# Which products of a Strassen-Winograd feed-forward block get their low weight part by an accumulating DMA

## The chip, the core and the metric

The kernel runs on one core of a Trainium2 chip. The metric is the device time in microseconds (us) of one execution: 2176.34 us before the change, the median of three runs (2171.39 to 2179.06).

Engines are called as the profile calls them: PE is TensorE, DVE is VectorE, ACT is ScalarE, POOL is GpSimd, SP is SyncE. SP issues the loads of weights, POOL the accumulating DMAs that this change is about; each has a queue of its own, and both queues use the same 16 DMA engines.

## The reference, cut to what matters

```python
# x (1, 512, 1024), DEPTH = 2 layers, D_FF = 2816, all float32
def swiglu(h, w_gu, w_down):
    gate, up = jnp.split(h @ w_gu, 2, axis=-1)
    return (jax.nn.silu(gate) * up) @ w_down

for l in range(DEPTH):
    x = x + 0.5 * swiglu(rmsnorm(x, g_ffn1[l]), w_ffn1_gu[l], w_ffn1_down[l])
    ...                       # conv heads, attention heads, cross-attention
    x = x + 0.5 * swiglu(rmsnorm(x, g_ffn2[l]), w_ffn2_gu[l], w_ffn2_down[l])
return rmsnorm(x, g_final)
```

The change touches the four feed-forward blocks (FFNs) alone: the products with w_gu (1024 x 5632, called gates) and with w_down (2816 x 1024, called down).

## The kernel before, in words

**Float32 in three passes.** PE multiplies a rounded form of float32. Each operand is therefore split into hi (the value rounded) and lo (value - hi), and each product is the sum of three matmuls, hi·hi, hi·lo and lo·hi.

**Products.** Most of an FFN is done in 2 x 2 blocks by the Strassen-Winograd scheme: seven products in place of eight, in the order `ORDER = (1, 7, 6, 2, 5, 4, 3)`. Product 1 takes the weight quadrant 11 as it is, product 2 the quadrant 21, product 3 the quadrant 22; products 7, 6, 5 and 4 take sums of quadrants, called T3, T2, T1 and T4: T3 = 22 - 12, T2 = T3 + 11, T1 = 12 - 11 (the code's signs), T4 = 21 - T2. DVE makes these sums (L83). Of the activations there are sums of the same kind.

A *gates chunk* has 512 columns of gate and as many of up; there are 20 such chunks, five to an FFN. A *unit* is the weight block of half a product, 128 x 1024 numbers, 512 KB. In the gates a unit feeds 12 matmuls with 512 moving columns (L216 in `mm3`, which other lines of the program use too). In a *down group* a unit feeds 24 matmuls with 256 moving columns (L658). There are eight big groups (two units of 24 a product) and three small ones (over three row blocks a quadrant: a unit of 24 and one of 12). Groups stand between chunks.

**Weights.** The class `Weights` brings them. `raw` lists a 512 KB load; `load` issues, on SP, as many as its limit of blocks outstanding allows, into the pool "big" of 12 buffers (L144); `free` gives a block back and calls `load`. `unit` lists a unit. `prefetch` makes the units, three ahead of the one that PE takes (`AHEAD = 3`, four buffers in the pool of units): hi by a cast on ACT (L164), then lo in one of two ways:

- on DVE: lo = source - hi (L169);
- by DMA (`keep == "dma"`): ACT writes -source into lo (L166, rounded as hi is), and POOL issues a DMA that adds the source to it in memory order (L167, `accum_op`). Its rows in the profile read wlo<-big.

Before, products 1, 2 and 3 take the second way everywhere, in gates and down groups alike: 186 accumulating DMAs.

**Order.** `ffn_plan` writes the order of chunks, transposes of activations (`turn`, L599), preparations of moving operands (`ready`) and products. `ready` makes a product's moving operand of activations: a sum on DVE (L630, L631, L637), hi by a cast on ACT (L644), lo on DVE (L645). Before, the `ready` of each product stands just ahead of the product that precedes it, and so it is issued while the product before that one runs on PE. In a big group the transposes of the next activations stand between product 1 and product 7. Each engine runs its instructions in order; semaphores between them are set by the framework, by tiles: who writes a tile waits until its readers are done, an accumulating DMA among them. An instruction that waits holds up everything behind it on its engine. A load on SP that writes a big buffer waits for the last reader of what the buffer held before.

Of the kernel before, what the change touches and what calls it, by code (L numbers as in the profile page):

```python
# [41 lines left out]
class Weights:  # L42
# [27 lines left out]
    def block(self, w, k0, nk, *cols):  # L70
        self.unit(self.raw(w, k0, nk, *cols))

    def quads(self, w, rows, cols, n):

        r, tmp = {}, {}
        parts = [(at, min(2, rows[0][1] - at)) for at in range(0, rows[0][1], 2)]

        def raw(q, h):
            at, nk = parts[h]
            r[q, h] = self.raw(w, rows[int(q[0]) - 1][0] + at, nk, (cols[int(q[1]) - 1], n))  # L80

        def tt(out, a, b, op):
            self.nc.vector.tensor_tensor(out=out, in0=a, in1=b, op=op)  # L83
            return out

        def block(q, h):
            return self.tiles[r[q, h]]

        def keep():
            pass  # L90

        def t3(h):
            tmp[h] = self.big((P, parts[h][1], n))
            return tt(tmp[h], block("22", h), block("12", h), ALU.subtract)

        def t2(h):
            return tt(tmp[h], tmp[h], block("11", h), ALU.add)

        def t1(h):
            return tt(block("12", h), block("12", h), block("11", h), ALU.subtract)  # L100

        def t4(h):
            return tt(tmp[h], block("21", h), tmp.pop(h), ALU.subtract)

        def freeing(*qs):
            return lambda: [self.free(r[q]) for q in qs]

        def product(i):
            for h in range(len(parts)):
                if i == 1:  # L110
                    raw("11", h)
                    self.unit(r["11", h], None, keep, "dma")
                elif i == 7:
                    raw("22", h)
                    raw("12", h)
                    self.unit(None, lambda h=h: t3(h), keep)
                elif i == 2:
                    raw("21", h)
                    self.unit(r["21", h], None, keep, "dma")
                elif i == 6:  # L120
                    self.unit(None, lambda h=h: t2(h), keep)
                elif i == 5:
                    self.unit(None, lambda h=h: t1(h), freeing(("11", h), ("12", h)))
                elif i == 4:
                    self.unit(None, lambda h=h: t4(h), freeing(("21", h)))
                else:
                    self.unit(r["22", h], None, freeing(("22", h)), "dma")

        return product

# [52 lines left out]
def trunk(ctx, tc, a, consts, out):  # L183
# [93 lines left out]
    for l in range(DEPTH):  # L277
        for which in (1, 2):
            gu, dn = a[f"w_ffn{which}_gu"][l], a[f"w_ffn{which}_down"][l]
            if which == 2:  # L280
                w_in, w_out = a["w_mix_in"][l], a["w_mix_out"][l]
                W.limit = 4
                for k in range(4):
                    W.block(w_in, 2 * k, 2, (2560, 512))
                for kind, i in MIX:
                    W.block(w_in, 0, KD, (MIX_COL[kind] + P * i, P))
                for c in range(KD):
                    W.block(a["w_xkv"][l], 0, KD, (P * c, P))
                for c in range(KD):
                    W.block(w_out, 0, KD, (P * c, P))  # L290
                for c in range(2):
                    for k in range(4):
                        W.block(a["w_xkv"][l], 2 * k, 2, (D + 512 * c, 512))
                W.limit = BIG_BUFS - 4
                for n in ("w_xq", "w_xo"):
                    for c in range(KD):
                        W.block(a[n][l], 0, KD, (P * c, P))
                W.slow = 10
            W.limit = BIG_BUFS - 2
            product = {}  # L300
            for op, c, i in ffn_plan(l == DEPTH - 1 and which == 2):
                if op == "plain":
                    c0 = P * FIRST[c]
                    W.block(gu, 2 * i, 2, (c0, 256), (DFF + c0, 256))
                elif op == "product":
                    if c not in product:
                        c0 = P * FIRST[c]
                        product[c] = W.quads(gu, ((0, 4), (4, 4)), (c0, DFF + c0), CHUNKS[c])
                    product[c](i)
                elif op == "group":  # L310
                    if c not in product:
                        product[c] = W.quads(dn, c, (0, 512), 512)
                    product[c](i)
                elif op == "down":
                    W.block(dn, FIRST[c], CHUNKS[c] // P, (256 * i, 256))
                elif op == "leave":
                    W.limit = 4
                    for e in range(4):
                        W.unit(W.raw(dn, FIRST[c] + 2 * (e % 2), 2, (512 * (e // 2), 512)), keep=True)
# [202 lines left out]
    def swiglu_half(n, after=None, early=None):  # L522
# [122 lines left out]
                nc.vector.tensor_tensor(out=lo, in0=o, in1=hi.bitcast(F32), op=ALU.subtract)  # L645
                made[c, i, p] = hi, lo

        def group(c, i, last):

            if i in (1, 7, 2):  # L650
                acc[CHAIN[i]] = [PS() for _ in range(2)]
# [1 line left out]
            for p, nk in pairs(c):  # L653
                w, z = W.take(), made.pop((c, i, p))
                for f in range(4):
                    for k in range(nk):
                        for q, (y, v) in enumerate(((0, 0), (0, 1), (1, 0))):
                            mm(  # L658
                                bank[f // 2][:, f % 2 * 256 : f % 2 * 256 + 256],
                                w[y][:, k, f * P : (f + 1) * P], z[v][:, k, :],  # L660
                                start=i in (1, 7, 2) and p == k == q == f % 2 == 0,
                                stop=2 * p + k == c[0][1] - 1 and q == 2,
                                skip_group_check=True,
                            )
            for half, tok in {
                1: ((0, 0),), 7: ((1, 1),), 6: ((0, 1),), 2: ((0, 0),), 5: ((1, 1),), 4: ((0, 1),), 3: ((1, 0),),
            }[i]:
                for b in range(2):
                    o = xx[2 * half + b][:, :, tok * 256 : tok * 256 + 256]
                    nc.vector.scalar_tensor_tensor(  # L670
                        out=o, in0=bank[b].rearrange("p (f t) -> p f t", f=2), scalar=0.5, in1=o,
                        op0=ALU.mult, op1=ALU.add,
                    )
# [62 lines left out]
        for at, (op, c, i) in enumerate(plan):  # L736
# [8 lines left out]
            elif op == "ready":  # L745
                ready(c, i)
            elif op == "group":
                group(c, i, after is not None and at >= len(plan) - 2 * len(ORDER))
            elif op == "down":
                down(c, i)  # L750
            else:
# [513 lines left out]
def ffn_plan(last):  # L1265
# [8 lines left out]
    def group(c, turn=None):  # L1274
# [3 lines left out]
        out.extend([("ready", c, 1), ("ready", c, 7), before, ops[0]])  # L1278
        if turn is not None:
            out.append(("turn", turn, 0))  # L1280
        for j in range(1, len(ORDER)):
            if j + 1 < len(ORDER):
                out.append(("ready", c, ORDER[j + 1]))
            out.append(ops[j])

    def both(c):

# [69 lines left out]
```

## Time and profile before

| what | value |
|---|---|
| median of three runs | 2176.34 us |
| the profiled execution | 2176.87 us, span 2175.1 us, mean granted clock 0.996 |
| PE busy | 2124.5 us, 98% |
| DVE busy | 1568.4 us, 72% |
| ACT busy | 1359.4 us, 62% |
| POOL busy | 258.9 us, 12% |
| accumulating DMAs (queue q0) | 95.17 MB, 23.8% of the 16 engines' span |
| loads (queue q1) | 212.88 MB, 31.4% of the 16 engines' span |

The span runs from the first to the last event on the core. Busy time is the sum of an engine's instructions. The releaser of a wait is what ended it. Issue to landing of a DMA is counted from the instruction that issues it to its last byte. PEclk is the granted clock of PE as a share of full speed.

### The profile page before, as it was taken

The numbers are of one execution on the slowest core, as the hardware profiler recorded it, in microseconds if no ns is written. First come the engines' busy times: TensorE is split into PE (matmuls) and PEld (weight loads), VectorE is DVE, ScalarE is ACT, GpSimd is POOL, SyncE is SP. The second block draws the span as 40 slices with busy tenths as digits, with TensorE's granted clock in tenths as the row PEclk, the third lists the DMA queues.
The fourth block names the chain that finished last, engine by engine and source line by source line (L and its number), as shares of the span: only waits on it lengthen the run. The fifth ranks groups of instructions, "written<-read, shape, count | busy, mean of one in ns | idle before, by whom it ended". The sixth has DMA issues, their size and how long they took to land. (4 is left out here: it accounts for less than half of the span.)

```text
span 2175.1 us, 30582 instructions
## 1 busy us (share of the span) xinstructions
PE 2124.5 (98%) x11602; PEld 1840.2 (85%) x11602; DVE 1568.4 (72%) x2196; ACT 1359.4 (62%) x1990; POOL 258.9 (12%) x293
## 2 busy tenths in 40 slices
PE   9999999999999999999999999999999999999998
PEld 7788989788888878898988898888888888788887
DVE  7687778668755667686886787777786547686775
ACT  7657676566544567667677666756664445576664
POOL 0111110022001011101101111101220010011010
PEclk9999999999999999999999999999999999999999
DMA  6776876123452256867757677742343422678662
GB/s 203 193 180 158 202 180 139 49 78 94 149 145 88 68 141 166 210 158 184 182 134 173 174 190 170 173 109 68 88 126 116 126 88 68 155 190 199 164 165 59
DMA packets 224186, 310.02 MB, mean 143 GB/s; under 512 B 12206, under 2 KB 128166, under 8 KB 224038
## 3 DMA queue, kind: packets, MB, share of 16 engines
q1 hardware_dynamic: 197222, 212.88, 31.4%
q0 software_dynamic: 26784, 95.17, 23.8%
q8 instruction: 91, 1.49, 0.3%
q14 instruction: 57, 0.47, 0.1%
q10 hardware_dynamic: 32, 0.01, 0.0%
HBM read 210.77 MB, written 2.10 MB: 98 GB/s over the span
## 5 line engine op out<-in xcount | busy, mean ns | idle before, releaser
L164 ACT CAST whi<-big 128x1024 fp32r<-128x1024 f32 x582 | 598.5, 1030 | 514.2 <-PE ps L216 221.0
L216 PE MATMUL ps<-whi,t 128*128 128x512 f32 x2624 | 816.2, 390 | 0.4 <-ACT t L220 0.2
L169 DVE TENSOR_TENSOR wlo<-big,whi 128x1024 fp32r<-128x1024 f32 (+1 forms) x396 | 478.1, 1207 | 222.1 <-ACT whi L164 218.0
L216 PEld LDWEIGHTS ps<-whi,t 128*128 128x128 f32 x2624 | 492.7, 188 | 102.7 <-ACT t L220 0.7
L216 PE MATMUL ps<-wlo,t 128*128 128x512 f32 x1312 | 512.4, 391 | 10.5 <-DMA wlo<-big 10.2
L216 PE MATMUL ps<-t,whi 128*128 128x512 f32 x1472 | 456.9, 391 | 1.5 <-ACT whi L855 1.5
L658 PE MATMUL ps<-t,whi 128*128 128x256 f32 x2296 | 423.6, 286 | 10.0 <-DVE t L645 7.8
L658 PEld LDWEIGHTS ps<-t,whi 128*128 128x128 f32 x2296 | 364.4, 194 | 13.3 <-DVE t L645 9.0
L658 PE MATMUL ps<-t,wlo 128*128 128x256 f32 x1148 | 327.6, 286 | 11.5 <-DMA wlo<-big 11.5
L83 DVE TENSOR_TENSOR big<-big 128x1024 f32<-128x1024 f32 x248 | 294.0, 1196 | 61.1 <-DMA wlo<-big 58.0
L216 PEld LDWEIGHTS ps<-t,whi 128*128 128x128 f32 x1472 | 274.5, 188 | 57.4 <-ACT whi L855 2.0
L167 POOL DMA_DIRECT2D wlo<-big x186 | 161.1, 866 | 1250.2 <-ACT wlo L166 636.5
L216 PEld LDWEIGHTS ps<-wlo,t 128*128 128x128 f32 x1312 | 246.4, 188 | 65.8 <-DMA wlo<-big 16.1
L216 PE MATMUL ps<-t,wlo 128*128 128x512 f32 x736 | 286.9, 390 | 1.1 <-DVE wlo L856 1.1
L658 PEld LDWEIGHTS ps<-t,wlo 128*128 128x128 f32 x1148 | 222.9, 194 | 13.1 <-DMA wlo<-big 13.1
L166 ACT ACTIVATE wlo<-big 128x1024 fp32r<-128x1024 f32 (+1 forms) x186 | 193.5, 1041 | 50.5 <-PE ps L216 49.5
L216 PEld LDWEIGHTS ps<-t,wlo 128*128 128x128 f32 x736 | 138.2, 188 | 30.5 <-DVE wlo L856 1.9
L670 DVE SCALAR_TENSOR_TENSOR x<-ps,x 128x512 f32<-128x512 f32 x154 | 103.9, 685 | 17.5 <-PE ps L658 16.9
L552 ACT COPY t<-ps 128x512 f32<-128x512 f32 x120 | 68.7, 587 | 31.0 <-PE ps L216 28.5
L926 POOL TENSOR_TENSOR t<-t,s 128x128 f32<-128x128 f32 (+1 forms) x64 | 60.2, 970 | 216.9 <-DVE s L924 182.2
L645 DVE TENSOR_TENSOR t<-t 128x512 fp32r<-128x512 f32 x88 | 57.0, 650 | 15.4 <-ACT t L644 15.1
L644 ACT CAST t<-t 128x512 fp32r<-128x512 f32 x88 | 51.1, 584 | 23.3 <-DVE t L631 15.3
(185 smaller groups left out, 1987.7 us busy)
## 6 DMA issues: line engine op xcount, KB each, us to landing
wlo<-big POOLq DMA_DIRECT2D x177, 512.0 KB, 5.1
big<-in_w_ffn_gu SPq DMA_DIRECT2D x160, 512.0 KB, 4.5
big<-in_w_ffn_down SPq DMA_DIRECT2D x80, 512.0 KB, 4.7
big<-in_w_mix_in SPq DMA_DIRECT2D x48, 512.0 KB, 4.0
big<-in_w_xkv SPq DMA_DIRECT2D x32, 512.0 KB, 3.9
big<-in_w_ffn_gu SPq DMA_DIRECT2D x32, 256.0 KB, 3.5
big<-in_w_mix_out SPq DMA_DIRECT2D x16, 512.0 KB, 4.6
big<-in_w_xq SPq DMA_DIRECT2D x16, 512.0 KB, 3.7
```

Source lines behind the costliest of these rows:

```text
L83: self.nc.vector.tensor_tensor(out=out, in0=a, in1=b, op=op)
L164: self.nc.scalar.copy(out=hi, in_=src)
L166: self.nc.scalar.activation(out=lo, in_=src, func=AF.Copy, scale=-1.0)
L167: self.nc.gpsimd.dma_start(out=lo, in_=src, accum_op=ALU.add)
L169: self.nc.vector.tensor_tensor(out=lo, in0=src, in1=hi.bitcast(F32), op=ALU.subtract)
L216: mm(ps, x, y, start=first and i == 0, stop=last and i == 2, skip_group_check=chained)
L552: nc.scalar.copy(out=s[i, e], in_=ps)
L644: nc.scalar.copy(out=hi, in_=o)
L645: nc.vector.tensor_tensor(out=lo, in0=o, in1=hi.bitcast(F32), op=ALU.subtract)
L658: mm(bank[f // 2][:, f % 2 * 256 : f % 2 * 256 + 256], w[y][:, k, f * P : (f + 1) * P], z[v][:, k, :], start=i in (1, 7, 2) and p == k == ...
L670: nc.vector.scalar_tensor_tensor(out=o, in0=bank[b].rearrange("p (f t) -> p f t", f=2), scalar=0.5, in1=o, op0=ALU.mult, op1=ALU.add,)
L926: nc.gpsimd.tensor_tensor(out=w[t], in0=w[t], in1=inv[:, t : t + 1].broadcast_to([P, (t + 1) * P]), op=ALU.mult)
```

## The change

1. `quads` takes a tuple `dma`: the products whose lo is made by the accumulating DMA. Gates chunks take (2, 3), down groups (6, 2, 5, 4, 3); every other product has its lo on DVE. In numbers: four accumulating DMAs to a gates chunk in place of six, ten to a group in place of six, 190 in all in place of 186.
2. The sums are written elsewhere. T2 goes over block 11, and T3's buffer is free from there on (before, T2 went over T3). T1 goes over block 12 as 22 - T2, T4 over block 11 as 21 - T2. Product 5 then gives back block 12 alone, product 4 blocks 21 and 11.
3. In groups, `ready` of the products 2, 5, 4 and 3 is issued in the middle of the product two before (after that product's first unit), by `group` itself. `ready` of 1, 7 and 6 stays where it was. The test for the last group counts the plan's entries anew, for `ready` entries no longer stand between the products.

The diff, without empty lines:

```diff
@@ -70,7 +70,10 @@
     def block(self, w, k0, nk, *cols):
         self.unit(self.raw(w, k0, nk, *cols))
-    def quads(self, w, rows, cols, n):
+    def quads(self, w, rows, cols, n, dma):
         r, tmp = {}, {}
         parts = [(at, min(2, rows[0][1] - at)) for at in range(0, rows[0][1], 2)]
@@ -94,37 +97,38 @@
             return tt(tmp[h], block("22", h), block("12", h), ALU.subtract)
         def t2(h):
-            return tt(tmp[h], tmp[h], block("11", h), ALU.add)
+            return tt(block("11", h), tmp.pop(h), block("11", h), ALU.add)
         def t1(h):
-            return tt(block("12", h), block("12", h), block("11", h), ALU.subtract)
+            return tt(block("12", h), block("22", h), block("11", h), ALU.subtract)
         def t4(h):
-            return tt(tmp[h], block("21", h), tmp.pop(h), ALU.subtract)
+            return tt(block("11", h), block("21", h), block("11", h), ALU.subtract)
         def freeing(*qs):
             return lambda: [self.free(r[q]) for q in qs]
         def product(i):
+            how = "dma" if i in dma else False
             for h in range(len(parts)):
                 if i == 1:
                     raw("11", h)
-                    self.unit(r["11", h], None, keep, "dma")
+                    self.unit(r["11", h], None, keep, how)
                 elif i == 7:
                     raw("22", h)
                     raw("12", h)
-                    self.unit(None, lambda h=h: t3(h), keep)
+                    self.unit(None, lambda h=h: t3(h), keep, how)
                 elif i == 2:
                     raw("21", h)
-                    self.unit(r["21", h], None, keep, "dma")
+                    self.unit(r["21", h], None, keep, how)
                 elif i == 6:
-                    self.unit(None, lambda h=h: t2(h), keep)
+                    self.unit(None, lambda h=h: t2(h), keep, how)
                 elif i == 5:
-                    self.unit(None, lambda h=h: t1(h), freeing(("11", h), ("12", h)))
+                    self.unit(None, lambda h=h: t1(h), freeing(("12", h)), how)
                 elif i == 4:
-                    self.unit(None, lambda h=h: t4(h), freeing(("21", h)))
+                    self.unit(None, lambda h=h: t4(h), freeing(("21", h), ("11", h)), how)
                 else:
-                    self.unit(r["22", h], None, freeing(("22", h)), "dma")
+                    self.unit(r["22", h], None, freeing(("22", h)), how)
         return product
@@ -305,11 +309,11 @@
                 elif op == "product":
                     if c not in product:
                         c0 = P * FIRST[c]
-                        product[c] = W.quads(gu, ((0, 4), (4, 4)), (c0, DFF + c0), CHUNKS[c])
+                        product[c] = W.quads(gu, ((0, 4), (4, 4)), (c0, DFF + c0), CHUNKS[c], (2, 3))
                     product[c](i)
                 elif op == "group":
                     if c not in product:
-                        product[c] = W.quads(dn, c, (0, 512), 512)
+                        product[c] = W.quads(dn, c, (0, 512), 512, (6, 2, 5, 4, 3))
                     product[c](i)
                 elif op == "down":
                     W.block(dn, FIRST[c], CHUNKS[c] // P, (256 * i, 256))
@@ -645,7 +649,7 @@
                 nc.vector.tensor_tensor(out=lo, in0=o, in1=hi.bitcast(F32), op=ALU.subtract)
                 made[c, i, p] = hi, lo
-        def group(c, i, last):
+        def group(c, i, last, then=None):
             if i in (1, 7, 2):
                 acc[CHAIN[i]] = [PS() for _ in range(2)]
@@ -662,6 +666,8 @@
                                 stop=2 * p + k == c[0][1] - 1 and q == 2,
                                 skip_group_check=True,
                             )
+                if then is not None and not p:
+                    ready(c, then)
             for half, tok in {
                 1: ((0, 0),), 7: ((1, 1),), 6: ((0, 1),), 2: ((0, 0),), 5: ((1, 1),), 4: ((0, 1),), 3: ((1, 0),),
             }[i]:
@@ -745,7 +751,11 @@
             elif op == "ready":
                 ready(c, i)
             elif op == "group":
-                group(c, i, after is not None and at >= len(plan) - 2 * len(ORDER))
+                j = ORDER.index(i) + 2
+                group(
+                    c, i, after is not None and at >= len(plan) - len(ORDER),
+                    ORDER[j] if 3 <= j < len(ORDER) else None,
+                )
             elif op == "down":
                 down(c, i)
             else:
@@ -1278,10 +1288,8 @@
         out.extend([("ready", c, 1), ("ready", c, 7), before, ops[0]])
         if turn is not None:
             out.append(("turn", turn, 0))
-        for j in range(1, len(ORDER)):
-            if j + 1 < len(ORDER):
-                out.append(("ready", c, ORDER[j + 1]))
-            out.append(ops[j])
+        out.append(("ready", c, ORDER[2]))
+        out.extend(ops[1:])
     def both(c):
```

**Where instructions stand now.** Three places, all in layer 0's first FFN, in the big group over chunks 2 and 3, or the one before and after it. "wlo_" is a lo of a unit, "big_" a 512 KB buffer or a sum written in one, t_ and r_ are activations; the numbers are those of tiles.

POOL's accumulating DMAs of this group, before: products 1, 2 and 3, two each.

```order
L167 DMA wlo_1861<-big_1457 128x1024
L167 DMA wlo_1904<-big_1490 128x1024
L167 DMA wlo_2077<-big_1783 128x1024
L167 DMA wlo_2116<-big_1806 128x1024
L167 DMA wlo_2297<-big_1735 128x1024
L167 DMA wlo_2342<-big_1762 128x1024
```

And of the change, products 6, 2, 5, 4 and 3:

```order
L171 DMA wlo_1970<-big_1469 128x1024
L171 DMA wlo_2046<-big_1490 128x1024
L171 DMA wlo_2083<-big_1802 128x1024
L171 DMA wlo_2114<-big_1804 128x1024
L171 DMA wlo_2154<-big_1758 128x1024
L171 DMA wlo_2190<-big_1779 128x1024
L171 DMA wlo_2230<-big_1469 128x1024
L171 DMA wlo_2266<-big_1490 128x1024
L171 DMA wlo_2311<-big_1733 128x1024
L171 DMA wlo_2344<-big_1777 128x1024
```

Product 1's two have gone, and ten stand where there were four; block buffers 1469 and 1490 occur twice, for T2 and T4.

SP's loads in the same stretch, before, with the semaphores that each waits for. DMASW0 to DMASW7 are counters that POOL's DMAs take in turn; in this group product 1 has 0 and 1, product 2 has 2 and 3, product 3 has 4 and 5, and 6 and 7 are older ones.

```order
L144 DMA big_2149<-in_w_ffn1_gu 128x2x512 [waits DMASW0_49,DMAHW3_49,DVE_49,Activation_49]
L144 DMA big_2151<-in_w_ffn1_gu 128x2x512 [waits DMASW1_49,DMAHW4_49,DVE_49,Activation_49]
L144 DMA big_2196<-in_w_ffn1_gu 128x2x512 [waits DMAHW5_49,DMASW2_49,DMAHW7_49,DVE_49,Activation_49]
L144 DMA big_2198<-in_w_ffn1_gu 128x2x512 [waits DMAHW6_49,DVE_49]
L144 DMA big_2229<-in_w_ffn1_gu 128x2x512 [waits DMAHW0_49,DMASW3_49]
L144 DMA big_2270<-in_w_ffn1_gu 128x2x512 [waits DVE_49]
L144 DMA big_2301<-in_w_ffn1_gu 128x2x512 [waits DMAHW1_49,DMASW6_49,DVE_49]
L144 DMA big_2346<-in_w_ffn1_gu 128x2x512 [waits DMAHW2_49,DMASW7_49,DVE_49]
```

And of the change, where product 6 has the counters 6 and 7, product 2 has 0 and 1, product 5 has 2 and 3, product 4 has 4 and 5, and product 3 has 6 and 7 again:

```order
L148 DMA big_2158<-in_w_ffn1_gu 128x2x512 [waits DMASW4_49,DMAHW3_49,DVE_49,Activation_49]
L148 DMA big_2194<-in_w_ffn1_gu 128x2x512 [waits DMASW5_49,DMAHW4_49,DVE_49,Activation_49]
L148 DMA big_2234<-in_w_ffn1_gu 128x2x512 [waits DMAHW5_49,DMASW0_49,DMAHW7_49,DVE_49,Activation_49]
L148 DMA big_2236<-in_w_ffn1_gu 128x2x512 [waits DMAHW0_49,DMASW1_49,DMAHW6_49,DVE_49,Activation_49]
L148 DMA big_2270<-in_w_ffn1_gu 128x2x512 [waits DMASW2_49,Activation_49]
L148 DMA big_2272<-in_w_ffn1_gu 128x2x512 [waits DMASW3_49,Activation_49]
L148 DMA big_2315<-in_w_ffn1_gu 128x2x512 [waits DMAHW1_49,DMASW4_49,Activation_49]
L148 DMA big_2348<-in_w_ffn1_gu 128x2x512 [waits DMAHW2_49,DMASW5_49,Activation_49]
```

Six loads in a row now wait for an accumulating DMA of the group's own, 0 to 5 in turn.

DVE around the moving operand of product 6, before (L630, L631 and L645 make it; L670 adds a bank of PE's sums to x; the two rows of L83 are T4's sums):

```order
L83 TENSOR_TENSOR big_1920<-big_1783,big_1920 128x1024 [waits DMAHW7_49,DVE_49]
L631 TENSOR_TENSOR t_2029<-t_2030,r_1630 128x512 [waits DVE_49]
L83 TENSOR_TENSOR big_1942<-big_1806,big_1942 128x1024 [waits DMAHW0_49]
L670 SCALAR_TENSOR_TENSOR x2_156<-ps_2045,x2_156 128x2x256 [waits PE_49]
L645 TENSOR_TENSOR t_2034<-t_2029,t_2033 128x512 [waits Activation_49]
L630 TENSOR_TENSOR t_2038<-r_1643,r_2021 128x512
L670 SCALAR_TENSOR_TENSOR x3_157<-ps_2046,x3_157 128x2x256 [waits PE_49]
L631 TENSOR_TENSOR t_2037<-t_2038,r_1643 128x512 [waits DVE_49]
L645 TENSOR_TENSOR t_2042<-t_2037,t_2041 128x512 [waits Activation_49]
```

And of the change:

```order
L635 TENSOR_TENSOR t_2026<-t_2027,r_1628 128x512 [waits DVE_49]
L86 TENSOR_TENSOR big_1469<-big_1802,big_1469 128x1024 [waits DMAHW7_49,DMASW6_49]
L649 TENSOR_TENSOR t_2031<-t_2026,t_2030 128x512 [waits Activation_49]
L634 TENSOR_TENSOR t_2035<-r_1641,r_2018 128x512
L676 SCALAR_TENSOR_TENSOR x2_156<-ps_2042,x2_156 128x2x256 [waits PE_49]
L635 TENSOR_TENSOR t_2034<-t_2035,r_1641 128x512 [waits DVE_49]
L86 TENSOR_TENSOR big_1490<-big_1804,big_1490 128x1024 [waits DMAHW0_49,DMASW7_49]
L676 SCALAR_TENSOR_TENSOR x3_157<-ps_2043,x3_157 128x2x256 [waits PE_49]
L649 TENSOR_TENSOR t_2039<-t_2034,t_2038 128x512 [waits Activation_49]
```

T4's two sums (L86, of block 21 and T2) stand there before as well, and now they wait for DMASW6 and DMASW7, product 6's accumulating DMAs, with the lo of product 6's operand (L649) behind them.

## Rows read from the trace of the kernel before

**Rows 1.** Page part 1: busy us of each engine (share of the span), instructions

```profile
PE 2124.5 (98%) x11602; PEld 1840.2 (85%) x11602; DVE 1568.4 (72%) x2196; ACT 1359.4 (62%) x1990; POOL 258.9 (12%) x293
```

**Rows 2.** What PE waited for: engine line <- releaser: us, times, longest

```profile
PE ps L658 <- DMA wlo<-big: 11.5, 8, 2.6
PE ps L216 <- DMA wlo<-big: 10.2, 11, 2.1
PE ps L658 <- DVE t L645: 7.8, 6, 1.3
...
PE ps L658 <- ACT t L644: 2.2, 4, 0.9
```

**Rows 3.** PE in L658, eleven group windows: us, busy (x), PEclk, DMA share, GB/s

```profile
332.62:367.69 35.07, 35.06 (x288) 34.76 (x288) 1.00 0.75 165
...
sum 399.45, PE 380.48 PEld 374.61; mean PE 34.59 PEld 34.06
```

**Rows 4.** Page part 5: busy us, mean ns of one | idle before, releaser

```profile
L164 ACT CAST whi<-big 128x1024 fp32r<-128x1024 f32 x582 | 598.5, 1030 | 514.2 <-PE ps L216 221.0
...
L169 DVE TENSOR_TENSOR wlo<-big,whi 128x1024 fp32r<-128x1024 f32 (+1 forms) x396 | 478.1, 1207 | 222.1 <-ACT whi L164 218.0
...
L83 DVE TENSOR_TENSOR big<-big 128x1024 f32<-128x1024 f32 x248 | 294.0, 1196 | 61.1 <-DMA wlo<-big 58.0
...
L166 ACT ACTIVATE wlo<-big 128x1024 fp32r<-128x1024 f32 (+1 forms) x186 | 193.5, 1041 | 50.5 <-PE ps L216 49.5
...
L645 DVE TENSOR_TENSOR t<-t 128x512 fp32r<-128x512 f32 x88 | 57.0, 650 | 15.4 <-ACT t L644 15.1
L644 ACT CAST t<-t 128x512 fp32r<-128x512 f32 x88 | 51.1, 584 | 23.3 <-DVE t L631 15.3
```

**Rows 5.** Page part 3: DMA queue, kind: packets, MB, share of 16 engines

```profile
q1 hardware_dynamic: 197222, 212.88, 31.4%
q0 software_dynamic: 26784, 95.17, 23.8%
```

**Rows 6.** Timeline of POOL, 1382 to 1398: start us, us, instruction [idle before]

```profile
1382.76 0.86 POOL L167 DMA_DIRECT2D wlo<-big  x1 [1.86 <-ACT wlo L166]
1385.47 0.86 POOL L167 DMA_DIRECT2D wlo<-big  x1 [1.86 <-DVE big L83]
1388.19 0.86 POOL L167 DMA_DIRECT2D wlo<-big  x1 [1.86 <-ACT wlo L166]
```

**Rows 7.** DMA issues at these three times: KB, us to landing

```profile
wlo<-big POOLq DMA_DIRECT2D x1, 512.0 KB, 5.0
...
wlo<-big POOLq DMA_DIRECT2D x1, 512.0 KB, 6.8
...
wlo<-big POOLq DMA_DIRECT2D x1, 512.0 KB, 9.0
```

**Rows 8.** Waits of SP's DMA queue, 1380 to 1390

```profile
SPq L144 <- DMA wlo<-big: 13.4, 2, 10.6
```

**Rows 9.** Windows: busy of PE, PEld, DVE, ACT, POOL, PEclk, DMA share, GB/s

```profile
1389.00:1391.00 2.00, 2.00 (x11) 1.65 (x10) 0.96 (x2) 2.00 (x3) 0.05 (x1) 1.00 1.13 228
1391.50:1392.50 1.00, 1.00 (x7) 0.84 (x6) 1.00 (x2) 0.00 (x0) 0.00 (x0) 1.00 0.99 363
```

**Rows 10.** PE's waits in 1878:1886, 2099:2108, 327:331 and 1396:1400

```profile
PE ps L216 <- DMA wlo<-big: 1.0, 1, 1.0
...
PE ps L216 <- DMA wlo<-big: 1.8, 2, 1.4
...
PE ps L658 <- DMA wlo<-big: 0.9, 1, 0.9
...
PE ps L658 <- DMA wlo<-big: 1.7, 1, 1.7
```

**Rows 11.** A gates window, all engines, 291 to 324

```profile
291.00:324.00 33.00, 33.00 (x150) 27.42 (x149) 24.04 (x28) 26.35 (x34) 5.22 (x6) 1.00 0.77 192
```

**Rows 12.** PE in L658 while its clock was at half

```profile
155.42:158.83 3.41, 3.41 (x18) 3.41 (x18) 0.50 1.03 195
```

## The prediction

> **What bounds the kernel now.** The first view is the page's busy line: TensorE (PE) is busy 2124.5 of 2175.1 us [rows 1], so the kernel ends where PE's work ends, and an edit is worth what it takes from PE's 50 us of idle time, or adds to it. The second is the list of what PE waited for [rows 2]. Read it by releaser: 21.7 us are waits for an accumulating DMA (wlo<-big: 11.5 in down groups, L658, and 10.2 in gates, L216), and 10.0 us are waits for the operand of a down group (7.8 for its lo on DVE, 2.2 for its hi on ACT). The third is PE in the down groups alone, in windows [rows 3]. An undisturbed big group runs its products 7 to 3, 288 matmuls, in 35.07 us, which is 0.1218 us a matmul and 2.92 us for a unit of 24. At that pace the eight big groups and the three small ones (252 matmuls, 30.69 us each) would take 372.6 us; they take 399.45, so 26.8 us are lost in them.
>
> **What a lo by DMA costs.** A unit's path is hi on ACT 1.03, -source on ACT 1.04, with an operand cast of 0.58 often between them [rows 4], then the DMA. The page's queue table prices the transfers [rows 5]: q0 carries only the 186 accumulating DMAs and takes 23.8% of the span of 16 engines, 2.78 us of all engines each; q1's 212.88 MB are 406 loads of 512 KB at 31.4%, 1.68 us each. So a load and an accumulating DMA together need 4.46 us of the engines, and a down unit gives them 2.92.
>
> What happens when they meet stands in one place of the trace. Accumulating DMAs are issued at 1382.76, 1385.47 and 1388.19, 2.7 us apart [rows 6], but land after 5.0, 6.8 and 9.0 us [rows 7], at 1387.8, 1392.3 and 1397.2: 4.5 and 4.9 us apart. In between SyncE waited twice for an accumulating DMA before it could issue the next load [rows 8]: each landing frees a buffer, a load starts into it, and the transfers follow each other. The throughput shows it too: 228 GB/s while one kind runs, 363 while the other does [rows 9], which is 2.30 and 1.44 us for 512 KB. That gives a lower bound of 3.74 us for the pair. The third of them kept PE waiting 1.7 us [rows 10].
>
> The Trainium skill (DMA: Bandwidth & Descriptors, Queues, rings and completion order) says that an engine changes between queues after a packet of some descriptors; the landings above follow each other as whole transfers.
>
> **Change part by part.**
>
> *Where the DMAs go.* Gates give up product 1's, 2 of 6 a chunk; down groups go from 6 (products 1, 2, 3) to 10 (6, 2, 5, 4, 3). The number hardly changes, 186 to 190, but ten now stand in a row. And the loads come to stand between them. T1 and T4 are now read by DMAs out of blocks 12 and 11, so these buffers come free at a landing: the load rows of a group wait for DMASW0 to DMASW5, the DMAs of products 2, 5 and 4, where before four of the eight waited for no DMA of their own group. So six units of each big group, from product 5's first to product 3's last, have a load in front.
>
> A unit has four buffers, so its hi starts when the unit three before it starts on PE: a lead of 8.77 us. The path is 1.03 + 0.58 + 1.04 + 5.0 = 7.65, which leaves 1.1 us. The first load finds the engines idle. The other five units each fall 4.46 - 2.92 = 1.54 us back, 7.7 in all, less 1.1: 6.6 us a group. By the lower bound of 3.74 it is 5 x 0.82 - 1.1 = 3.0. I take 5.2, nearer the upper end, since the landings seen were 4.5 and 4.9 apart. Eight groups: 41.6 us (24 to 53).
>
> By the Trainium skill's fit for one such DMA (same page, Anatomy of one DMA: about 2.0 us + bytes / 436 GB/s) 512 KB would be 3.2 us in all, an estimate, 1.2 of them transfer, and nothing would be late. The landings of 5.0 and more and the 2.78 us of [rows 5] speak against it; what it would mean is the first rival.
>
> *Small groups (three).* Their units alternate between 24 and 12 matmuls, 2.92 and 1.46 us, 4.38 a product. A first unit's lead is 2.92 + 1.46 + 1.46 = 5.84, its path at least 7.07: 1.2 us late at product 6. For products 5 and 4 the engines have 1.5 x 2.78 + 2 x 1.68 = 7.5 us of work (half a transfer taken as half the time) where PE needs 4.38: 6.2 back, less 1.1 of slack. Sum 6.3 a group, 18.9 in all (9 to 24).
>
> *Sums in other tiles.* T4 is written over block 11, which T2's DMA reads. So DVE stops at the T4 sums until product 6's DMAs land, and behind them stand an eviction and the lo of product 6's second operand: 1.20 + 0.65 us [rows 4] after the landing. Before, six big groups waited about 1.7 us at this very place (10.0 us, rows 2). I take 1.5 us in all eight, 12 us (0 to 20). T3's buffer is free earlier, which only brings two loads forward.
>
> *Operands half a product earlier.* They are made at the middle of the product two before, not at the start of the one before. PE waits only for product 6's, whose place is unchanged (behind the transposes, ahead of product 7); the others waited for nothing. Worth 0; the casts now stand between hi and lo on ACT, which is in the path above.
>
> *Product 1 on DVE.* Its waits end: 1.0 and 1.8 us in gates and 0.9 and 1.7 in groups [rows 10], with the 0.16 us that PE's pipeline hides before each of the six: -6.4 us. Price: two lo of 1.21 us a product on DVE, hidden under gates where DVE is busy 24.04 of 33 us [rows 11]; without that cover 2.4 us a chunk, and T3 of the next chunk, which waits for product 3's landing, is where it would go first. Product 2's waits in gates stay.
>
> *Clock.* PE's clock fell to half for 3.41 us four times in mid-kernel, each time within 2 us of such a wait; 18 matmuls are run there [rows 12] in place of 28: 1.2 us each. I keep that as it is (-5 to +10).
>
> **Sum.** After: 41.6 + 18.9 + 12 = 72.5 us lost in the groups, in place of 26.8: +45.7. With -6.4 it is +39.3 on the profiled execution's 2176.87 us (span 2175.1 and 1.8 around it; the median of the runs is 2176.34): **2216 us**.
>
> **Rivals.**
>
> *Faster: the DMAs hide.* If the engines took an accumulating DMA in under 2.92 us beside the loads, or served them ahead of the loads, nothing of the six units would be late. Then all DMA waits in groups end (11.5 us, which holds the 2.6 of product 1), those of product 1 in gates (2.8), half of the operand waits (5) and the clock dips (4.8): 24.1 us, **2153 us**. For it: DMA is far from busy on average, q0 and q1 together 55%, and trains of four accumulating DMAs without loads cause no wait. Against it: the landings. It decides at a spacing of 2.92 us. The skill's fit above would bring it about. 14%.
>
> *No change: it cancels.* At a spacing of 3.74, with the loads slipping behind the group's last units, a tail costs 2 us: 16 + 3 x 3.7 as now + 0 of operand waits, 27 against 26.8, less 6.4: about 2171 to 2178. 9%.
>
> *Worse: the queue behind T4.* If product 6's DMA lands with a load ahead (6.8, not 5.0 us), DVE's in-order queue stands still 1.8 us longer in each of eight groups, 14 us, and more than ten waits of over 1 us a FFN bring the clock down in each group, 11 x 1.2 = 13 us: **2243 us**. 15%.
>
> **How the numbers follow.** Forecast 62%, with a range of its own from 2185 to 2235 (24 and 53 for the tails, 9 and 24 for the small groups). Faster 14%, cancelled 9%, worse 15%. A measurement of this kernel can tell about 0.3%, 6.5 us, from no change. Faster by more: 14% and a little of the cancelled case, 0.15. Within: 0.08. Slower: 0.77. Leaving out the fast rival and the far end of the worse one, the range is 2168 to 2250.
>
> **What would show it.** Right: PE's waits in L658's successor for wlo<-big rise from 11.5 to some 55 us, in series of 1 to 1.6 us 4.4 us apart at products 4 and 3 of every group, and accumulating DMAs there land after 7 to 9 us; a big group's 288 matmuls take 41 to 42 us, a small group about 37; SyncE's loads wait for wlo<-big; no DMA wait remains in product 1. Wrong: group windows at 35 to 36 us, landings 2.9 us or less apart beside loads, or a new wait at the start of a gates chunk for a lo on DVE, which would put the cost on the cover that I counted as free.

## The result and the profile after

The changed kernel takes 2247.62 us (median of four runs, 2245.36 to 2247.77) against 2174.74 before: a ratio of 1.0327, 95% interval [1.0314, 1.034], some 73 us slower. The forecast was 2216 in a range of 2168 to 2250, so the direction and the range held (the range by 2 us at its top), but the time lies next to the worst rival's 2243. The profiled execution spans 2245.9 us, 70.8 more than before.

Where the 70.8 us are is read from two lines of each kernel. First the busy line of the page, after:

```profile
PE 2149.5 (96%) x11602; PEld 1860.7 (83%) x11602; DVE 1562.1 (70%) x2192; ACT 1361.0 (61%) x1994; POOL 262.6 (12%) x297
```

The same 11602 matmuls take PE 25.0 us more than in [rows 1], so part of the loss is no wait at all. Then what PE waited for (us in total, times, longest):

```profile
PE ps L662 <- DMA wlo<-big: 55.5, 35, 4.4
PE ps L662 <- DVE t L649: 19.2, 10, 3.1
...
PE ps L220 <- DMA wlo<-big: 2.4, 2, 1.8
...
PE ps L662 <- ACT t L648: 0.3, 1, 0.3
```

Against [rows 2]: in the groups +44.0 for the accumulating DMAs, +11.4 and -1.9 for operands; in the gates -7.8. That is +45.7, and with the 25.0 it makes the 70.7 of the span. Most of the 25.0 is the clock. PE in L662, the eleven groups one by one (us, PE busy, PEld busy, granted clock, DMA share, GB/s):

```profile
121.31:166.75 45.44, 35.23 (x252) 34.41 (x251) 0.89 0.77 180
214.77:259.75 44.98, 36.81 (x288) 34.98 (x288) 1.00 0.87 206
...
1091.01:1136.71 45.70, 38.88 (x288) 37.52 (x288) 0.93 0.96 235
...
1328.88:1372.50 43.62, 37.83 (x288) 36.40 (x288) 0.96 0.90 213
1457.70:1499.18 41.48, 36.38 (x288) 34.95 (x288) 1.00 0.95 208
...
sum 481.80, PE 406.36 PEld 393.38; mean PE 36.94 PEld 35.76
```

The sum was 399.45 with 380.48 busy [rows 3]. So the groups took 82.4 us more, 56.5 as waits (+53.5 from the list above and 2.6 that lay in product 1 of big groups before, outside these windows) and 25.9 in busy time. Where the clock column is below 1, most of that is the clock. It is not all: the groups at 214.77 and 1457.70 ran at 1.00, and PE is busy 1.8 and 1.3 us longer in them than the 35.06 of [rows 3]. It stopped five times in the second, so a stop costs about a quarter of a us of busy time beside the wait itself. The clock stood at half in 15 stretches of the trace (61.4 us together, the one at the program's end left out) in place of four (13.7 us). Each of the 15 begins in the last 1.2 us of a wait of 1.7 to 4.4 us, or within 1.6 us after one. One of them lies right behind a wait of 2.3 us in a small group:

```profile
147.07:150.48 3.41, 3.41 (x19) 3.41 (x18) 0.00 (x0) 0.00 (x0) 0.00 (x0) 0.50 1.03 173
```

PE is busy throughout, and runs 19 matmuls where 28 would have fitted.

Of what the forecast wanted to see, a big group's 288 matmuls take 41.5 to 45.7 us (41 to 42 said), a small group 41.8 to 45.4 (37 said), and product 1 waits for no DMA any more. The waits of the big groups begin earlier than said: 13.7 us stand at product 5, 7.5 at product 4 and 6.7 at product 3, the longest 3.0.

The DMAs of one big group's tail, issued from 1347 to 1370 (KB, median us to landing):

```profile
big<-in_w_ffn_gu SPq DMA_DIRECT2D x5, 512.0 KB, 10.0
wlo<-big POOLq DMA_DIRECT2D x5, 512.0 KB, 8.8
```

and the throughput there (busy of PE, PEld, DVE, ACT, POOL; clock, DMA share, GB/s):

```profile
1352.00:1356.00 4.00, 1.94 (x16) 1.73 (x15) 1.29 (x2) 3.59 (x5) 0.86 (x1) 1.00 1.06 263
1356.00:1360.00 4.00, 3.83 (x32) 3.62 (x31) 1.98 (x3) 1.52 (x2) 0.86 (x1) 1.00 1.07 218
```

The DMA engines are full, the accumulating DMAs land after 8.8 us in place of 5.1 (the page's median before), and the loads slow down as much: 10.0 us where 4.7 is the page's median (4.5 before). The two queues do not share in one way all the time. From 1357 to 1359, and then from 1364 to 1366 (packets, MB, share of the 16 engines):

```profile
q0 software_dynamic: 118, 0.42, 105.6%
q1 hardware_dynamic: 10, 0.02, 2.6%
...
q1 hardware_dynamic: 233, 0.44, 58.9%
q0 software_dynamic: 60, 0.20, 50.5%
```

The prediction had read [rows 7] as whole transfers that follow each other. The Trainium skill (DMA: Bandwidth & Descriptors, Queues, rings and completion order) has the engines change between queues in small pieces, of a packet. The second of these windows agrees with it, for both kinds move forward together there; in the first the accumulating DMAs have the engines nearly alone, though a load was issued at 1355.69 and landed only at 1365.7. What decides between the two was not found.

The other wait, at product 6, is on DVE's timeline (start, us, operation, idle before and its releaser):

```profile
1331.84 0.69 DVE L635 TENSOR_TENSOR t<-t,r 128x512 f32<-128x512 f32 x1
1335.44 1.22 DVE L86 TENSOR_TENSOR big<-big 128x1024 f32<-128x1024 f32 x1 [2.91 <-DMA wlo<-big]
1336.59 0.68 DVE L649 TENSOR_TENSOR t<-t 128x512 fp32r<-128x512 f32 x1
```

T4's sum (L86) holds DVE for 2.91 us until product 6's DMA has landed, and the lo of product 6's operand (L649) stands behind it; PE waited 2.3 us for that.

### The profile page after: what moved, and what is told of

Same layout as the page of the kernel before. It is cut to its first block, busy times and chain, and to the rows that moved or that the text cites. A ratio compares the mean times of both kernels' runs of the same rounds, so it can differ in the third digit from the quotient of the medians.

```text
span 2245.9 us, 30440 instructions
## 1 busy us (share of the span) xinstructions
PE 2149.5 (96%) x11602; PEld 1860.7 (83%) x11602; DVE 1562.1 (70%) x2192; ACT 1361.0 (61%) x1994; POOL 262.6 (12%) x297
## 5 line engine op out<-in xcount | busy, mean ns | idle before, releaser
L662 PE MATMUL ps<-t,whi 128*128 128x256 f32 x2296 | 440.7, 293 | 19.6 <-DVE t L649 19.2
L662 PEld LDWEIGHTS ps<-t,whi 128*128 128x128 f32 x2296 | 378.0, 201 | 22.8 <-DVE t L649 21.5
L662 PE MATMUL ps<-t,wlo 128*128 128x256 f32 x1148 | 340.4, 296 | 55.9 <-DMA wlo<-big 55.5
L86 DVE TENSOR_TENSOR big<-big 128x1024 f32<-128x1024 f32 x248 | 291.4, 1193 | 111.6 <-DMA wlo<-big 106.8
L220 PEld LDWEIGHTS ps<-t,whi 128*128 128x128 f32 x1472 | 274.5, 188 | 57.3 <-ACT whi L865 2.0
L662 PEld LDWEIGHTS ps<-t,wlo 128*128 128x128 f32 x1148 | 231.1, 201 | 64.1 <-DMA wlo<-big 64.0
L220 PEld LDWEIGHTS ps<-t,wlo 128*128 128x128 f32 x736 | 138.1, 188 | 30.5 <-DVE wlo L866 1.9
L391 POOL TENSOR_TENSOR s<-s,mhalf 128x4 f32<-128x4 f32 (+1 forms) x19 | 18.3, 961 | 477.2 <-DVE s L388 439.3
```

Source lines behind the costliest of these rows:

```text
L220: mm(ps, x, y, start=first and i == 0, stop=last and i == 2, skip_group_check=chained)
L662: mm(bank[f // 2][:, f % 2 * 256 : f % 2 * 256 + 256], w[y][:, k, f * P : (f + 1) * P], z[v][:, k, :], start=i in (1, 7, 2) and p == k == ...
```

## The experiments

Theory A: ten accumulating DMAs in a group share the DMA engines with the loads that they set off, product 6's hold up T4's sums on DVE, and PE's clock falls at the waits. Rivals B and C: the cost lies in the sums T, or in the earlier operands. Others are named where they are tested. Every ratio is against the kernel before on the same chip.

**One part of the change at a time.** Four kernels on the base of the one before.

The placement alone (all products get `how` as product 1 does here, and the gates' chunks take (2, 3)):

```diff
+            how = "dma" if i in dma else False
...
-                    self.unit(r["11", h], None, keep, "dma")
+                    self.unit(r["11", h], None, keep, how)
...
-                        product[c] = W.quads(dn, c, (0, 512), 512)
+                        product[c] = W.quads(dn, c, (0, 512), 512, (6, 2, 5, 4, 3))
```

> The kernel before with the new placement of accumulating DMAs alone (gates 2, 3; groups 6, 2, 5, 4, 3), sums and operands as before. Theory A (the ten DMAs of a group cost the time: they share the DMA engines with the loads that they trigger, product 6's hold up T4's sums on DVE, and PE's clock falls at the waits): 2230 to 2260 us, waits of PE in groups for wlo<-big of 45 to 65 us (55.5 in the change), for operands on DVE 14 to 24 (19.2), and ten or more falls of the clock. Here T4 is written over T2's own buffer, which product 6's DMA reads too, so T4's sums wait just as they do in the change. Rival B (the sums in other tiles make the loads wait for DMAs): 2175 to 2205. Rival C (operands made earlier delay -source on ACT): 2200 to 2225.

Measured: 2269.9 us, ratio 1.0451 [1.0434, 1.0468], more than the whole change.

```profile
PE ps L659 <- DMA wlo<-big: 59.4, 42, 4.1
PE ps L659 <- DVE t L646: 21.7, 8, 4.4
PE ps L217 <- DMA wlo<-big: 9.7, 7, 2.6
```

The placement carries all of the loss; both waits of the groups are there in full with the old sums and operands. The time is 10 us above what was expected; the gates' line shows the most of it: 9.7 us in place of the change's 2.4.

The sums alone (T1, T4 and the blocks given back as in the change):

```diff
-            return tt(tmp[h], tmp[h], block("11", h), ALU.add)
+            return tt(block("11", h), tmp.pop(h), block("11", h), ALU.add)
```

> The kernel before with the sums T written over other tiles alone; accumulating DMAs for products 1, 2, 3 as before. Theory A: within 6 us of before, 2169 to 2181. Rival B: slower by 20 us or more, since blocks 11 and 12 come free at other times and loads wait. Rival C: within 6 us.

Measured: 2179.24, ratio 1.0033 [1.0019, 1.0046]: 7 us slower, small and just clear of nothing. Rival B has fallen as the cause of 73 us.

The operands alone:

```diff
+                if then is not None and not p:
+                    ready(c, then)
```

> The kernel before with the operands of products 2, 5, 4 and 3 of the groups made half a product earlier, alone. Theory A: within 6 us of before (2169 to 2181), the waits for operands of product 6 unchanged at about 10 us. Rival B: the same. Rival C: slower by 20 us or more.

Measured: 2174.28, ratio 1.0004 [0.9994, 1.0014]: nothing. Rival C has fallen.

The gates' part of the placement alone:

```diff
-                        product[c] = W.quads(gu, ((0, 4), (4, 4)), (c0, DFF + c0), CHUNKS[c])
+                        product[c] = W.quads(gu, ((0, 4), (4, 4)), (c0, DFF + c0), CHUNKS[c], (2, 3))
...
-                        product[c] = W.quads(dn, c, (0, 512), 512)
+                        product[c] = W.quads(dn, c, (0, 512), 512, (1, 2, 3))
```

> The kernel before with product 1 of the gates on DVE alone (gates 2, 3; groups 1, 2, 3). Theory A: faster by the waits of product 1 in gates, 3 to 8 us: 2167 to 2172, no wait for wlo<-big in product 1 of a gates chunk, those in product 2 stay. Rival D (DVE was the cover and is now late in gates): slower by 5 to 48 us (up to 2.4 us in each of 20 chunks), with PE waiting for a lo on DVE.

Measured: 2172.36, ratio 0.9997 [0.9985, 1.0008]. Both expectations missed: no new wait for a lo on DVE, and no gain. The gates' waits were all in product 2 now, and the line was hardly shorter than the 10.2 of [rows 2] (the profiled execution took 2180.02 us, 8 above the median):

```profile
PE ps L217 <- DMA wlo<-big: 9.3, 8, 2.9
```

**Which of the other parts gives back 22 us.** The change with the operands made where they were:

```diff
-        out.append(("ready", c, ORDER[2]))
-        out.extend(ops[1:])
+        for j in range(1, len(ORDER)):
+            if j + 1 < len(ORDER):
+                out.append(("ready", c, ORDER[j + 1]))
+            out.append(ops[j])
```

> The changed kernel with the operands of groups made where they were before (DMA placement and sums of the change). The placement alone took 2269.9 us, the whole change 2247.6, so sums and operands together give back 22. If the operands made earlier give it back (the casts no longer stand between hi and -source of a product that is late): 2262 to 2275. If the sums do (two buffers free earlier, loads sooner): 2243 to 2253. In between, both.

Measured: 2248.15, ratio 1.0343 [1.0326, 1.036], as the whole change. So the sums in other tiles take 22 us off the new placement, though alone they cost 7. In the profiles of this run and of the placement alone, 8.6 of the 16.9 us between the spans are waits in gates (9.7 to 1.1), 7.6 waits in groups (81.1 to 73.5).

**Product 6 off the DMA.** On the change:

```diff
-                        product[c] = W.quads(dn, c, (0, 512), 512, (6, 2, 5, 4, 3))
+                        product[c] = W.quads(dn, c, (0, 512), 512, (2, 5, 4, 3))
```

> The changed kernel with product 6 of the groups on DVE again (groups 2, 5, 4, 3). Theory A: T4's sums wait for no accumulating DMA, so PE's waits for operands of product 6 fall from 19.2 to 8 to 13 us (10.0 before), the small groups' waits at product 6 (3.6, 2.9 and 2.9 us) go, waits in groups for wlo<-big fall from 55.5 to 35 to 48 us, since the tail of products 5, 4, 3 stays: 2210 to 2232 us. Rival F (product 6 is late in any case, its lo on DVE stands behind the sums): waits at product 6 stay under another name, 2240 us or more. Rival G (product 6's DMAs are the root and the tail only follows from the delay that they start): waits for wlo<-big below 25 us, under 2205.

Measured: 2215.46, ratio 1.0185 [1.0169, 1.02].

```profile
PE ps L662 <- DMA wlo<-big: 42.8, 36, 3.7
PE ps L662 <- DVE t L649: 7.7, 14, 1.3
```

32 us less. In the profiles, 36.1: 12.7 of DMA waits, 11.5 of operand waits, and 11.9 of PE's busy time, with 8 stretches of half clock in place of 15. Rivals F and G have fallen; the tail stays, as A has it.

**Loads out of the groups.** On the change; `load` does nothing while `hold` is set, from product 6 until product 4's sums are in x, and each load that was held waits for a copy of one element of x:

```diff
+            if self.late is not None:
+                self.nc.vector.tensor_copy(out=t[:, 0, :1], in_=self.late)
...
+            if i == 6 and c[0][0] != FIRST[4]:
+                W.hold = True
...
+            if i == 4:
+                W.hold, W.late = False, xx[0][:, 0, 256:257]
+                W.load()
+                W.late = None
```

> The changed kernel with the loads that the products of a group would trigger held back until product 4 has been added to x, in the eight groups that a gates chunk or down block follows within the FFN (the three groups that end an FFN keep theirs); each such load waits for a DVE copy of one element. Theory A (loads and accumulating DMAs of one group hold each other up): in these eight groups the waits for wlo<-big fall from 44 us (of 55.5; 11 are in the other three) to under 20, and the time to 2205 to 2228, some of it given back at the start of the next chunk. Rival E (ten accumulating DMAs in a row are too late by their own length and the lead of four unit buffers, loads or not): 35 us or more remain, 2238 us or more.

Measured: 2199.18, ratio 1.0115 [1.0098, 1.0132]: 48 us less than the change, below what was expected.

```profile
PE ps L667 <- DMA wlo<-big: 23.3, 20, 3.3
PE ps L667 <- DVE t L652: 17.0, 11, 2.9
...
PE ps L223 <- DVE wlo L176: 2.9, 4, 0.8
```

Of the 23.3, 12.7 are in the three groups that keep their loads. The five big groups with held loads wait 0.7 us together, where the change waited 17.4; the three small ones 9.9, where it waited 26.9. All stretches of half clock but the program's last lie in two of the three groups that keep theirs. The same big group in both kernels, all its DMAs, first the change (1328 to 1373):

```profile
q0 software_dynamic: 1440, 5.24, 59.5%
q1 hardware_dynamic: 2155, 4.15, 28.5%
...
wlo<-big POOLq DMA_DIRECT2D x10, 512.0 KB, 7.2
big<-in_w_ffn_gu SPq DMA_DIRECT2D x7, 512.0 KB, 10.0
```

and with held loads (1295 to 1340):

```profile
wlo<-big POOLq DMA_DIRECT2D x10, 512.0 KB, 4.6
big<-in_w_ffn_gu SPq DMA_DIRECT2D x9, 512.0 KB, 7.6
```

The same ten DMAs land after 4.6 us in place of 7.2 once the loads are held back. Rival E has fallen for big groups. In small groups about 3.3 us of each group's wait stay without loads, so there the row of DMAs and the short lead cost something by themselves.

**The clock.** On the change; `still` is a tile of zeros:

```diff
+            fill = {6: 24 if small else 16, 5: 16 if small else 0, 3: 24 if small else 0}.get(i, 0)
...
+                for _ in range(fill if not p else 0):
+                    mm(bank[0][:, :256], still[:, :P], still, start=False, stop=False, skip_group_check=True)
```

> The changed kernel with matmuls on zeros (added into the bank in use, so they change no value) ahead of the first unit of product 6 (24 in small groups, 16 in big) and in small groups of products 5 (16) and 3 (24): 320 matmuls, 39 us at 0.122 us each, where PE waits some 46 us in the changed kernel. Theory A (the clock falls because PE stands still there): falls of the clock go from 15 windows to 8 or fewer, and the time to 2228 to 2243 in spite of the added work. Rival H (the falls have another cause, the work filled in is simply added where it doesn't fit): 13 windows or more, and 2248 to 2290 us.

Measured: 2246.01, ratio 1.0329 [1.0313, 1.0344].

```profile
PE 2168.9 (97%) x11922; PEld 1880.2 (84%) x11922; DVE 1561.4 (70%) x2193; ACT 1361.5 (61%) x1994; POOL 262.1 (12%) x297
```

The time missed the expected range by 3 us at the top; the clock did as A says: 4 stretches at half in place of 15. The 320 added matmuls are 39.0 us, yet PE's busy time rose by only 19.4, so the clock gave back 19.6 for 47.8 us less at half; waits in groups fell from 75.0 to 52.9. The work that was filled in paid for itself, and no more.

**Can the placement be had without its costs?** Four kernels, in which loads are held, product 6 is off the DMA, or the down groups run product 2 ahead of product 6, so that the product after the transposes needs no sum of activations.

The order alone, on the kernel before (`ready` follows `DOWN`):

```diff
+DOWN = (1, 7, 2, 6, 5, 4, 3)
-        ops = [("group", c, i) for i in ORDER]
+        ops = [("group", c, i) for i in DOWN]
```

> The kernel before with the down groups' products in the order 1, 7, 2, 6, 5, 4, 3 (gates unchanged): product 2, whose operand needs no sum, comes right after the transposes, product 6 after it. Of the 10.0 us of operand waits before (all at product 6) under 4 should remain: 2162 to 2170 us. Rival: product 2's lo by DMA is now needed one product sooner with the same lead, and its wait takes the place: 2171 to 2180 us.

Measured: 2184.2, ratio 1.0049 [1.0036, 1.0062]: slower, by more than the rival said.

```profile
PE ps L659 <- DMA wlo<-big: 19.5, 15, 2.8
PE ps L217 <- DMA wlo<-big: 8.8, 9, 2.1
PE ps L659 <- DVE x L671: 8.1, 8, 1.1
```

The operand waits have gone, but the DMAs are late (11.5 to 19.5 us: 5.0 of the 8.0 more at product 2, 3.2 at product 3), and a new wait has come at product 5 in the big groups. Product 5 now follows product 6 directly and adds into the same bank, so it waits until DVE has added product 6's sums to x (L671).

The same with `hold`, whose diff stands above:

> The same, and the loads of eight groups held until product 4 is added, as in the run with held loads. Theory A: waits for wlo<-big in groups fall from 11.5 us to under 7: 2158 to 2168. Rival: three DMA products in seven leave room enough for the loads, and holding them only delays the next chunk: 2169 to 2182.

Measured: 2229.41, ratio 1.0264 [1.0248, 1.028]: far outside both.

```profile
PE ps L220 <- DMA wlo<-big: 42.2, 24, 4.3
PE ps L664 <- DMA wlo<-big: 14.7, 13, 2.6
```

The held loads now meet the accumulating DMAs of product 1 of the next gates chunk, which the change has moved to DVE: 8.8 us of waits in gates become 42.2, 34.5 of them in product 1. This is theory A once more, in another place: whatever DMA stands beside a burst of loads is late.

The change with groups (2, 5, 4, 3) and `hold`, first with the order of products as it was, then with `DOWN`; both edits stand above:

> The changed kernel with groups 2, 5, 4, 3 by DMA and held loads, order of products as it was. Theory A: product 6 on DVE takes off what it took off without held loads at the operands (from 17 to about 8 us), and the eight groups' waits for wlo<-big stay at 10 or below: 2182 to 2193 us. Rival (the two remedies take off the same thing): 2195 to 2203.

> The changed kernel with groups 2, 5, 4, 3 by DMA, held loads and the order 1, 7, 2, 6, 5, 4, 3 together. Theory A (the three costs are the loads beside the DMAs, product 6's DMAs ahead of T4's sums, and the clock at the waits; they are separate): waits for operands under 5 us, waits for wlo<-big in groups 12 to 22, six or fewer falls of the clock: 2174 to 2188 us. Rival (the tails come back in the three groups that keep their loads and at product 2, which now comes first): 2190 to 2210.

Measured: 2188.14, ratio 1.0064 [1.005, 1.0077], and 2180.32, ratio 1.0036 [1.0024, 1.0048]. Operand waits were 7.9 us in the first, and none in the second; waits for wlo<-big in groups 22.0 and, above the expected 22, 26.0. Both times lie in the ranges of theory A, though the eight groups with held loads still wait 11.7 us for wlo<-big in the first, where 10 or less was expected. The two remedies do not simply add up: held loads alone took 48 us off the change, product 6 alone 32, both together 59, so part of the loss goes with either. With loads held and product 6 on DVE the new placement comes within 16 us of the kernel before, with the other order too within 8. No kernel that was run beats it.

## Why the prediction was right in direction and short in size

- *Tails of big groups.* Right in mechanism: loads and accumulating DMAs hold each other up, shown by the run with held loads (17.4 to 0.7 us). The size was too large: 41.6 us forecast, 28.6 measured (55.5 less 26.9 in small groups), 3.6 a group where I took 5.2. Of the two bounds, the lower (3.0) was the nearer. The term that was too large is the spacing, 4.46 us, and 4.5 to 4.9 by the landings that I preferred. In the tail shown above, the DMA issued at 1344.47 landed after 5.4 us, and the fifth behind it, issued at 1360.79, after 8.8: five landings in 19.7 us, 3.9 each. In that time (1349.8 to 1369.6) nearly one load moved for each DMA:

```profile
q0 software_dynamic: 720, 2.62, 67.0%
q1 hardware_dynamic: 1284, 2.48, 35.5%
```

- *Small groups.* Right in kind, too small: 18.9 forecast, 26.9 measured (10.2, 7.7, 9.0), above the range's 24. Most of the excess is at product 6: 9.4 us, where 1.2 a group was forecast.
- *Product 6 and T4.* The wait was foreseen on the right engine and at the right place: 12 forecast, 19.5 measured, inside the range of 20. The reason was half right. T4's sums do wait for product 6's DMA, and taking that away took PE's wait back to 7.7; but the new tile has no part in it: with the old sums, where T4 overwrites T2's own buffer, the wait is as long (21.7).
- *The three together:* 72.5 forecast, 75.0 measured as waits. The sum is good by luck: a term too large covers two too small.
- *What was taken off.* The forecast set these 72.5 us of waits against the 26.8 us lost before. Of the 26.8, 7.9 are busy time of PE (380.48 less 372.6 at full pace), which the clock term was to keep. Waits against waits would have been +53.5 in place of +45.7, and the forecast 2224.
- *The clock.* The step that failed. "I keep that as it is (-5 to +10)" measured +25.0 us of busy time, some 20 of them the clock. The forecast itself put 11.5 us of DMA waits up to some 55, and had noted that each fall stood next to such a wait; it should have scaled the falls with the waits. The price was small as well: 1.2 us for a fall of 3.41 us, where the run with matmuls filled in had 47.8 us less at half clock, which is 14 times 3.41, and got back 19.6, 1.4 each. The Trainium skill (TensorE: Matmul & The Clock Gate, Terms) puts the penalty at the throttled time by the share withheld: an estimate of 23.9 us for the 47.8. The 19.6 lie below it. The other 5 of the 25.0 fit the stops of PE named above (an estimate: PE waited 71 times in place of 51, at a quarter of a us each). The rival "queue behind T4" had the clock in it (13 us), and came to 2243 by it. That the falls follow the waits is shown by the run with matmuls filled in: 4 falls in place of 15.
- *Product 1 on DVE.* -6.4 forecast for gates and groups, -7.8 measured in the gates alone, but by another cause: alone, product 1 on DVE gives nothing (ratio 0.9997), since product 2's waits take its place. With the new placement it is the sums that bring the gates' waits from 9.7 to 1.1; why they help there and cost 7 us alone was not settled.
- *Operands earlier:* priced at 0, and 0 both alone (1.0004) and within the change (2248.15 against 2247.62).
- *The faster rival* had asked for a spacing below 2.92 us beside loads. With held loads the DMAs of big groups do land in time, so what it lacked was room without loads, not a faster DMA.

## What to carry to other kernels

Moving work from an engine to a DMA queue moves it next to whatever else the DMA engines do just then: count transfers stretch by stretch, and look at what each landing sets free, since a buffer freed by a landing starts a load that meets the next DMA. Before an accumulating DMA is put on a tile, look at who writes that tile next, and what stands behind that write in its engine's queue. And when a forecast adds waits to a busy PE, let the falls of the clock grow with them.

## What had not been expected of the hardware

- Beside five accumulating DMAs, loads of 512 KB took 10.0 us to land in place of 4.7, and the DMAs 8.8 in place of 5.1. For 2 us the DMAs had 105.6% of the engines and the loads 2.6%; for another 2 us it was 50.5% and 58.9%.
- A stop of PE cost about a quarter of a us of busy time beside the wait (1.3 us more for five stops at clock 1.00).
- The clock stood at half for 61.4 us in 15 stretches with 75 us of waits in groups, and for 13.7 us in four once 22 of the 75 us of waits were filled; each such us cost about 0.4 us.
